# Six more weight slabs of a hybrid decoder block in the seven-product scheme, with its activation differences kept longer and one projection moved behind another

## The chip, the cores and the metric

The kernel runs on one core of a Trainium2 chip. The metric is the time of one execution on the device in microseconds (us). The kernel before took 943.69, 945.80 and 946.13 us in three runs, a median of 945.8. One further execution was profiled. Engines are called as in the profile: PE is TensorE, PEld its weight loads, DVE is VectorE, ACT is ScalarE, POOL is GpSimd, SP issues the transfers.

## What is computed

One layer on 512 tokens and 16 meta tokens (T = 528), model width 1024, all in float32. The input is normalised, multiplied by one wide matrix `w_in`, and cut into eight parts of 1024 columns. Four feed a retention branch, two a gated linear recurrence, two the gates by which the branches are mixed. A feed-forward network (FFN) follows.

```python
u = rmsnorm(h, mix_norm_w)
proj = u @ w_in
q, k, v, g_ret, lru_in, lru_gate, gate_a, gate_b = split(proj, split_at)
o = chunk_retention(rotary(q), rotary(k), v)            # normalised per head
y_ret = (silu(g_ret) * o) @ w_branch_ret
c = causal_depthwise_conv(lru_in, conv_w, conv_b)
r = rg_lru(c, lru_wa, lru_ba, lru_wx, lru_bx, lru_lambda)
y_lru = (gelu(lru_gate) * r) @ w_branch_lru
mixed = sigmoid(gate_a) * y_ret + sigmoid(gate_b) * y_lru
h = h + mixed @ w_out
u = rmsnorm(h, ffn_norm_w)
g, up = split(u @ w_ffn_in)
h = h + (silu(g) * up) @ w_ffn_out
```

In `rg_lru`, two small block-diagonal products of `c` give two sigmoid gates, from which the decay and the input of a recurrence over the tokens are made.

## The kernel before, in words

**Precision.** A float32 product is made of three: each operand is split into `hi` (rounded, by ACT, L290) and `lo` (the rest, by DVE, L294), and PE sums hi x hi, hi x lo and lo x hi into PSUM (`block`, L372 to L374, or `mm3`, L362 to L364).

**Weights.** A slab is 256 output columns of a weight matrix. It comes in four quarters of 128x512 elements: two halves of the depth, two halves of the columns. SP loads a quarter into one of eight `raw` buffers, ACT and DVE split it into one of nine pairs of `hi` and `lo`. `emit` does this for one piece; `weights` calls it up to eight pieces ahead of the one that PE uses next, in the order of the list `pieces`.

**Two ways to multiply a slab with the activations** (two halves of the depth by two halves of the tokens: `b11`, `b21`, `b12`, `b22`):

- Plain (`plain`, `plain512`): four pieces, eight blocks of 12 matmuls. A column half has one PSUM bank, which ACT reads at the end through the slab's function.
- Seven products (`fast`, `fast512`, and `fast528` where the meta tokens are wanted too), a Strassen scheme: POOL makes four sums of quarters, `s1` to `s4` (L260, `combine`), which with the quarters `a11`, `a12` and `a22` are seven pieces. PE multiplies them with four activation blocks or with the differences `t1` to `t4`, in seven blocks of 12 matmuls. After four blocks ACT copies two of the banks (L392, L394) and DVE adds one (`pz`, L393); only then may the last three blocks be summed into the same banks. At the end ACT copies one (L398), and DVE makes the result with two adds (L407, L408).

`t1` to `t4` are made once (`sums_of`), with hi and lo in eight of 32 slots of SBUF that all larger tiles share (`Slots`, `get`, `put`).

**Order of the work.** `PLAN` lists it. R0 to R3 are the retention's projections, A0 to A3 the gate `gate_a`, BR the product with `w_branch_ret`. I0 to I3 are the recurrence's input (`lru_in`), T0 to T3 its small gates and then its steps, L0 to L3 the gate `lru_gate`, B0 to B3 the gate `gate_b`, BL the product with `w_branch_lru`. In the trace these are the tiles `li`, `gt`, `lg` and `gate`, `w_br` and `w_bl`; a number behind li, lg or gate in the orders below counts the slabs of `w_in` (li16 is I0, lg20 is L0, gate28 is B0). The FFN's first product has `f` and `zwf`, `yxf`, its second `fo`.

Work of DVE, ACT and POOL that follows a projection is put off (`defer`) and mixed into PE's later work by `tick`: the convolution of an input slab (`conv`: per half of the slab one L978, three L980, one split at L422) and the recurrence (`recurrence`: POOL's L1019 and L1045, ACT's lookups, DVE's L1033 to L1047 and the product with the gate, L1052). Within an engine the build's scheduler then sets the order.

**Who is plain before.** K0 and G0, I2 and I3, L0 to L3, B0 to B3 (L217), and the first two FFN slabs. `t1` to `t4` are given back at BR.

Of the kernel before, what the change touches and what calls it, by code (L numbers as in the profile page):

```python
# [13 lines left out]
AF = mybir.ActivationFunctionType  # L14
# [6 lines left out]
SEQ = 512  # L21
# [41 lines left out]
FIRST_LOADS = "w0 x1 w1 m w2 w3 x2 x3"  # L63


PLAN = "R0 R1 R2 R3 A0 A1 A2 A3 I0 I1 BR T0 L0 I2 T1 L1 I3 L2 T2 B0 L3 T3 B1 B2 B3 BL"

PLAIN_R = "K0 G0".split()
NORM = 2.0
SUM = 2.0  # L70

# [39 lines left out]
class Slots:  # L111
# [12 lines left out]
    def get(self, n=SEQ, dt=F32):  # L124
        if n <= T and dt == F32:
            if self.halves:
                slot, i = self.halves.pop(0)
            else:
                slot, i = [*self.open(dt), 0], 0
                self.halves.append((slot, 1))  # L130
            slot[2] += 1
            t = slot[1][:, i * T:i * T + n]
            self.held[id(t)] = (t, slot, i)
        else:
            tag, mem = self.open(dt)
            t = mem[:, :n]
            self.held[id(t)] = (t, tag, None)
        return t

    def put(self, *tiles):  # L140
        for t in tiles:
            _, slot, i = self.held.pop(id(t))
            if i is None:
                self.free.append(slot)
                continue
            slot[2] -= 1
            self.halves.append((slot, i))
            if slot[2] == 0:
                self.halves = [h for h in self.halves if h[0] is not slot]
                self.free.append(slot[0])  # L150
# [3 lines left out]
def hybrid_block(ctx: ExitStack, tc: tile.TileContext, a: dict):  # L154
# [8 lines left out]
    get, put = slots.get, slots.put  # L163

    def bank(name):
        return ps.tile([P, 512], F32, tag="ps", name=name)
# [24 lines left out]
    Q, K, V, G, LI, LG, GA, GB = (4 * i for i in range(8))  # L191
# [4 lines left out]
    SLAB_OF = {"I": ("w_in", LI), "L": ("w_in", LG), "A": ("w_in", GA), "B": ("w_in", GB), "T": ("gates", 0)}  # L196
    for step in PLAN.split():
        if step in ("BR", "BL"):
            order += [(f"w_{step.lower()}", hf) for hf in range(2)]
        elif step[0] == "R":  # L200
            s = int(step[1])
# [12 lines left out]

    def plain_slab(key, i):
        if key == "w_in":
            return i in [{"Q": Q, "K": K, "G": G}[r[0]] + int(r[1]) for r in PLAIN_R] or LI + 2 <= i < GA or i >= GB  # L217
        return key == "w_fi" and i < FIRST

    pieces = []  # L220
# [18 lines left out]
    def behind(ins, other):  # L239

        if other is not None:
            tc.add_manual_dep(ins.ins, other.ins.name, mybir.DependencyInfo(
                mybir.DependencyClass.NoSync, mybir.DependencyReason.DATA), reason="issue order")
        return ins
# [74 lines left out]
    def lookup(*args, **kw):  # L319
        state["table"] = behind(nc.scalar.activation(*args, **kw), state.get("table"))  # L320
# [56 lines left out]
    def fast(key, s, X, n, banks, name):  # L377

        z, w_, y, x = banks
        own = n == TH
        ws = small.tile([P, TH], F32, tag="ws", name=f"ws{name}{s}")
        pz = small.tile([P, 2, TH], F32, tag="pz", name=f"pz{name}{s}")
        u2 = small.tile([P, TH], F32, tag="u2", name=f"u2{name}{s}")
        part = lambda name: weights((key, s, name))[0]
        block(z, part("s1"), X["t1"], n, True)
        block(w_, part("s3"), X["t3"], n, own)
        block(y, part("a12"), X["b21"], n, True)  # L390
        block(x, part("a11"), X["b11"], n, own)
        nc.scalar.copy(ws[:, :n], w_)  # L392
        nc.vector.tensor_tensor(pz[:, 1, :n], z, ws[:, :n], op=ALU.add)  # L393
        nc.scalar.copy(pz[:, 0, :n], x)  # L394
        block(z, part("s4"), X["b22"], n, False)
        block(w_, part("a22"), X["t4"], n, False)
        block(x, part("s2"), X["t2"], n, False)
        nc.scalar.copy(u2[:, :n], x)  # L398
        return pz, u2

    def fast512(key, s, X, out, name):

        zw, yx = bank(f"zw{name}{s}"), bank(f"yx{name}{s}")
        pz, u2 = fast(key, s, X, 256, (zw[:, :256], zw[:, 256:], yx[:, :256], yx[:, 256:]), name)
        out = out.rearrange("p (q n) -> p q n", n=256)
        halves = lambda t: t.rearrange("p (q n) -> p q n", n=256)
        nc.vector.tensor_tensor(out[:, 0::3], halves(yx), pz[:, :, :256], op=ALU.add)  # L407
        nc.vector.tensor_tensor(out[:, 1:3], halves(zw), u2[:, :256].unsqueeze(1).broadcast_to([P, 2, 256]), op=ALU.add)  # L408
# [25 lines left out]
    def plain(s, n, outs):  # L434


        shared = n == 256
        for j in range(2):
            for i, part in enumerate(PLAIN[2 * j:2 * j + 2]):
                w = weights(("w_in", s, part))[0]  # L440
                for h in range(2):
                    block(outs[j][h], w, UV[("b11", "b12", "b21", "b22")[2 * i + h]], n, i == 0 and (h == 0 or not shared))

    def plain512(s, name):

        pbs = [bank(f"{name}{s}_{j}") for j in range(2)]
        plain(s, 256, [(pb[:, :256], pb[:, 256:]) for pb in pbs])
        return pbs

    def branch(key, source, done):  # L450


        parts = {}
        for hf in range(2):
            acc = [bank(f"{key}{hf}_{c}") for c in range(4)]
            for k in range(KT):
                i = k // 2
                if i not in parts:
                    f = source(i)
                    parts[i] = get(D, F32R), get(D, F32R)  # L460
                    split(parts[i], f)
                    put(f)
                w = weights((key, i, k % 2 + 2 * (1 - hf)))[0]
                xh, xl = (p[:, k % 2 * SEQ:(k % 2 + 1) * SEQ] for p in parts[i])
                for c in range(4):
                    mm3(acc[c], *(p[:, c * P:(c + 1) * P] for p in w), xh, xl, k == 0, k == KT - 1)
                if hf == 1 and k % 2 == 1:
                    put(*parts.pop(i))
            for c in range(4):
                done(4 * hf + c, acc[c])  # L470
# [25 lines left out]
    def blocks_of(n):  # L496

        F = {b: get(4 * TH) for b in BLOCKS.values()}
        X = {b: (get(4 * TH, F32R), get(4 * TH, F32R)) for b in BLOCKS.values()}
        v4 = lambda t: t[:, :4 * n].rearrange("p (k t) -> p k t", k=4)  # L500
        return F, X, {b: v4(t) for b, t in F.items()}, {b: tuple(v4(t) for t in x) for b, x in X.items()}
# [40 lines left out]
    UF, U, UFV, UV = blocks_of(TH)  # L542
    for load in FIRST_LOADS.split():
        if load[0] == "w":
            key, i, c = pieces[int(load[1:])]
# [384 lines left out]
    def gated(T, base):  # L930


        def done(c, pb):
            s, j = c // 2, c % 2
            if j == 0:
                T[s] = get(D)
            sl = slice(j * SEQ, (j + 1) * SEQ)
            nc.vector.scalar_tensor_tensor(T[s][:, sl], sig[base, s][:, sl], 1.0, pb, ALU.add, ALU.mult)
            if j == 1:
                put(sig.pop((base, s)))  # L940
        return done

    def retained(i):
        for item in ret[i]:
            finish(item)
        return R[i]
# [108 lines left out]

    def lru_gate(s):
        x = get(D)
        for j, pb in enumerate(plain512(LG + s, "lg")):
            lookup(x[:, j * SEQ:(j + 1) * SEQ], pb, AF.Gelu_apprx_tanh)
        Z[s] = x  # L1060


# [20 lines left out]

    plan = PLAN.split()
    for step in plan:
        s = int(step[1]) if step[1:2].isdigit() else None
        if step[0] == "R":
            ret_project(s)
            if s == 0:
                softplus()  # L1090
            if s == 3:
                put(ropef)
        elif step == "BR":
            for i in range(4):
                retained(i)
            for b in ("t1", "t2", "t3", "t4"):
                put(*U.pop(b))
            branch("w_br", lambda i: R[i], gated(macc, GA))
        elif step == "BL":
            for b in ("b11", "b12", "b21", "b22"):  # L1100
                put(*U.pop(b))
            branch("w_bl", recurred, merged)
        elif step[0] == "A":
            gate(s, GA)
        elif step[0] == "B":
            gate(s, GB)
        else:
            {"I": lru_in, "T": lru_gates, "L": lru_gate}[step[0]](*(int(i) for i in step[1:]))
# [7 lines left out]
    def out_norm(t):  # L1116
# [3 lines left out]
        else:  # L1120
            diag, rows = None, get(D)
            held = rows
            nc.vector.tensor_scalar_mul(rows, h_sb[t], rms_factors(h_sb[t], f"h{t}", diagonal=False))
        yield NORM
        for c in range(2):
# [206 lines left out]
```

## Time and profile before

| what | value |
|---|---|
| three runs | 943.69, 945.80, 946.13 us |
| the profiled execution | 945.7 us, its span 943.9 us |
| granted PE clock, mean | 0.989 |
| busy in the span: PE, DVE, ACT, POOL | 918.9, 701.9, 468.7, 362.9 us |
| instructions | 16975 |
| moved by DMA | 91.5 MB, a mean of 97 GB/s |

A share of busy time is a mean over stages with different limits. The 40 slices of the page are 23.6 us each; a digit is the busy share in tenths. The recurrence's part, which the change edits, lies at about 304 to 536 us of the span.

### The profile page before, as it was taken

The page shows a single profiled execution, that of the slowest core. Times are in us where ns is not written, and L with a number is a line of the kernel's source. Part 1 is how long each engine was busy: PE and PEld are TensorE (multiplying, and loading weights), DVE is VectorE, ACT ScalarE, POOL GpSimd, SP SyncE. Part 2 cuts the span into 40 slices and gives each one's busy share as a digit, 9 for nine tenths or more (in the row PEclk, how much of TensorE's full clock was granted, in tenths as well). Part 3 has the DMA queues.
Part 4 walks back from the last instruction along what each step waited for, and adds up shares of the span by engine and source line. Part 5 has one row for each costly group of instructions (what it writes and reads, how often), then busy time and mean ns, then how long its engine had stood idle before and what let it go on. Part 6 is the DMA issues. An engine that isn't in the chain of part 4 may idle for free.

```text
span 943.9 us, 16975 instructions
## 1 busy us (share of the span) xinstructions
PE 918.9 (97%) x6562; PEld 862.7 (91%) x6562; DVE 701.9 (74%) x927; ACT 468.7 (50%) x823; POOL 362.9 (38%) x259
## 2 busy tenths in 40 slices
PE   8999899988999999999999999999999999999996
PEld 8999899988999889999998888999999999888885
DVE  5878996999788846887744527999999999832223
ACT  6654544545456327747933324554555556622213
POOL 6144654547351002112100214587887785000003
PEclk9999999999999999999999999999999999999999
DMA  7141122222123332232442222133333233432202
GB/s 276 57 141 62 57 85 85 74 84 68 56 80 124 122 102 79 84 108 91 147 132 90 93 87 78 56 111 104 102 98 124 92 99 124 135 102 91 88 1 90
DMA packets 48498, 91.50 MB, mean 97 GB/s; under 512 B 5520, under 2 KB 5648, under 8 KB 48416
## 3 DMA queue, kind: packets, MB, share of 16 engines
q1 hardware_dynamic: 46976, 86.70, 28.5%
q10 hardware_dynamic: 1440, 3.71, 1.2%
q8 instruction: 51, 0.84, 0.4%
q14 instruction: 31, 0.25, 0.1%
HBM read 88.29 MB, written 2.10 MB: 96 GB/s over the span
## 4 chain that ended last, share of the span: by engine, by line
PE 90%; DVE 6%; issue 2%; ACT 1%; DMA 0%; POOL 0%; POOLq 0%; DVEq 0%; ACTq 0%
PE fo L362 4%; PE fo L364 4%; PE fo L363 4%; PE zwf L372 4%; PE zwf L374 4%; PE zwf L373 4%; DVE lo L294 3%; PE yxf L372 3%; PE yxf L374 3%; PE yxf L373 3%; PE lg L374 2%; PE gate L374 2%; PE gate L372 2%; PE lg L372 2%; PE lg L373 2%; PE gate L373 2%
## 5 line engine op out<-in xcount | busy, mean ns | idle before, releaser
L294 DVE TENSOR_TENSOR lo<-raw_w_in,hi 128x512 fp32r<-128x512 f32 x96 | 82.6, 866 | 30.0 <-ACT hi L290 29.8
L372 PE MATMUL zwf<-b,hi 128*128 128x256 f32 x320 | 91.5, 287 | 2.2 <-DVE pzf L393 2.2
L373 PE MATMUL zwf<-b,hi 128*128 128x256 f32 x320 | 90.1, 282 | 0.0
L374 PE MATMUL zwf<-b,lo 128*128 128x256 f32 x320 | 90.0, 281 | 0.0
L294 DVE TENSOR_TENSOR lo<-s_w_fi,hi 128x512 fp32r<-128x512 f32 x80 | 83.8, 1084 | 1.3 <-ACT hi L290 0.8
L290 ACT CAST hi<-raw_w_in 128x512 fp32r<-128x512 f32 x96 | 58.9, 619 | 46.8 <-PE w_br L363 13.9
L294 DVE TENSOR_TENSOR lo<-raw_w_fo,hi 128x512 fp32r<-128x512 f32 x44 | 30.3, 692 | 64.4 <-ACT hi L290 64.4
L294 DVE TENSOR_TENSOR lo<-s_w_in,hi 128x512 fp32r<-128x512 f32 x64 | 64.3, 1014 | 11.8 <-ACT hi L290 9.5
L260 POOL TENSOR_TENSOR s_w_fi<-raw_w_fi,raw_w_fi 128x512 f32<-128x512 f32 x40 | 69.0, 1744 | 8.2 <-DVE lo L294 8.2
L362 PE MATMUL fo<-hi,b 128*128 128x512 f32 x176 | 69.4, 394 | 0.0
L363 PE MATMUL fo<-lo,b 128*128 128x512 f32 x176 | 68.8, 391 | 0.0
L364 PE MATMUL fo<-hi,b 128*128 128x512 f32 x176 | 68.2, 394 | 0.0
L294 DVE TENSOR_TENSOR lo<-raw_w_fi,hi 128x512 fp32r<-128x512 f32 x46 | 67.8, 1501 | 0.0
L372 PE MATMUL yxf<-b,hi 128*128 128x256 f32 x240 | 65.5, 281 | 2.2 <-ACT pzf L394 2.2
L373 PE MATMUL yxf<-b,hi 128*128 128x256 f32 x240 | 66.7, 280 | 0.0
L374 PE MATMUL yxf<-b,lo 128*128 128x256 f32 x240 | 66.6, 281 | 0.0
L372 PEld LDWEIGHTS zwf<-b,hi 128*128 128x128 f32 x320 | 60.7, 190 | 4.5 <-DVE pzf L393 3.2
L290 ACT CAST hi<-raw_w_fo 128x512 fp32r<-128x512 f32 x44 | 27.3, 621 | 73.7 <-PE fo L364 71.2
L290 ACT CAST hi<-s_w_in 128x512 fp32r<-128x512 f32 x64 | 39.6, 620 | 46.4 <-PE zwgate L373 8.0
L260 POOL TENSOR_TENSOR s_w_in<-raw_w_in,raw_w_in 128x512 f32<-128x512 f32 x32 | 46.2, 1452 | 42.1 <-DMA raw_w_in<-in_w_in 26.0
L374 PEld LDWEIGHTS zwf<-b,lo 128*128 128x128 f32 x320 | 61.0, 191 | 0.0
L373 PEld LDWEIGHTS zwf<-b,hi 128*128 128x128 f32 x320 | 60.9, 190 | 0.0
(412 smaller groups left out, 3312.0 us busy)
## 6 DMA issues: line engine op xcount, KB each, us to landing
raw_w_in<-in_w_in SPq DMA_DIRECT2D x112, 256.0 KB, 3.1
raw_w_fi<-in_w_fi SPq DMA_DIRECT2D x88, 256.0 KB, 3.3
raw_w_fo<-in_w_fo SPq DMA_DIRECT2D x44, 256.0 KB, 2.9
raw_w_v<-in_w_v SPq DMA_DIRECT2D x16, 256.0 KB, 4.6
raw_w_br<-in_w_br SPq DMA_DIRECT2D x16, 256.0 KB, 3.0
raw_w_bl<-in_w_bl SPq DMA_DIRECT2D x16, 256.0 KB, 3.0
raw_w_out<-in_w_out SPq DMA_DIRECT2D x16, 256.0 KB, 2.9
b<-in_x SPq DMA_DIRECT2D x4, 512.0 KB, 6.5
```

Of the source, the lines that this page charges most:

```text
L260: behind(nc.gpsimd.tensor_tensor(sums[key, i, name], x, y, op=op), state.get("diag"))
L290: nc.scalar.copy(hi, src)
L294: engine.tensor_tensor(lo, src, hi.bitcast(F32), op=ALU.subtract)
L362: nc.tensor.matmul(out, wh, xh, start=start, stop=False, skip_group_check=True)
L363: nc.tensor.matmul(out, wh, xl, start=False, stop=False, skip_group_check=True)
L364: nc.tensor.matmul(out, wl, xh, start=False, stop=stop, skip_group_check=True)
L372: nc.tensor.matmul(out, wh, xh, start=start and i == 0, stop=False, skip_group_check=True)
L373: nc.tensor.matmul(out, wh, xl, start=False, stop=False, skip_group_check=True)
L374: nc.tensor.matmul(out, wl, xh, start=False, stop=i == 3, skip_group_check=True)
```

## The change

Four places are edited.

- `PLAIN_L` names the plain slabs of the recurrence's part: I2, I3, L3 and B0 stay plain. L0, L1, L2, B1, B2 and B3 go over to seven products.
- `lru_gate` gets the branch for it: `fast512` into an SBUF tile, then one lookup of 1024 columns in place of two of 512. `gate`, for B, has this branch already.
- `t1` to `t4` are given back at BL, no longer at BR.
- I1 stands behind BR in the plan, no longer ahead of it.

```diff
-PLAN = "R0 R1 R2 R3 A0 A1 A2 A3 I0 I1 BR T0 L0 I2 T1 L1 I3 L2 T2 B0 L3 T3 B1 B2 B3 BL"
+PLAN = "R0 R1 R2 R3 A0 A1 A2 A3 I0 BR I1 T0 L0 I2 T1 L1 I3 L2 T2 B0 L3 T3 B1 B2 B3 BL"
 
 PLAIN_R = "K0 G0".split()
+
+PLAIN_L = "I2 I3 L3 B0".split()
...
     def plain_slab(key, i):
         if key == "w_in":
-            return i in [{"Q": Q, "K": K, "G": G}[r[0]] + int(r[1]) for r in PLAIN_R] or LI + 2 <= i < GA or i >= GB
+            return i in [{"Q": Q, "K": K, "G": G}[r[0]] + int(r[1]) for r in PLAIN_R] or i in [{"I": LI, "L": LG, "B": GB}[r[0]] + int(r[1]) for r in PLAIN_L]
...
     def lru_gate(s):
         x = get(D)
-        for j, pb in enumerate(plain512(LG + s, "lg")):
-            lookup(x[:, j * SEQ:(j + 1) * SEQ], pb, AF.Gelu_apprx_tanh)
+        if plain_slab("w_in", LG + s):
+            for j, pb in enumerate(plain512(LG + s, "lg")):
+                lookup(x[:, j * SEQ:(j + 1) * SEQ], pb, AF.Gelu_apprx_tanh)
+        else:
+            fast512("w_in", LG + s, UV, x, "lg")
+            lookup(x, x, AF.Gelu_apprx_tanh)
         Z[s] = x
...
         elif step == "BR":
             for i in range(4):
                 retained(i)
-            for b in ("t1", "t2", "t3", "t4"):
-                put(*U.pop(b))
             branch("w_br", lambda i: R[i], gated(macc, GA))
         elif step == "BL":
-            for b in ("b11", "b12", "b21", "b22"):
+            for b in list(U):
                 put(*U.pop(b))
             branch("w_bl", recurred, merged)
```

The orders of the two built programs differ on PE from the last blocks of I0 and the first of w_br to the first pass of w_bl; ahead of that and behind it they are the same. In sum the change has 72 matmuls of 128x256 fewer. DVE has 36 instructions more (18 lo, 6 pz, 12 adds), ACT 30 more (18 casts, 18 copies of 128x256, 6 lookups fewer), POOL 24 sums more. The transfers are as many as before.

In the orders shown below, source lines of the change are two higher than in the kernel before (L296 for L294, L395 for L393), `b` with a number is a tile in SBUF, and the number behind an underscore only counts tiles.

## Prediction

> **What bounds the kernel now.** I read the page first, for who is busy where.
>
> ```profile
> PE 918.9 (97%) x6562; PEld 862.7 (91%) x6562; DVE 701.9 (74%) x927; ACT 468.7 (50%) x823; POOL 362.9 (38%) x259
> PE   8999899988999999999999999999999999999996
> DVE  5878996999788846887744527999999999832223
> PE 90%; DVE 6%; issue 2%; ACT 1%; DMA 0%; POOL 0%; POOLq 0%; DVEq 0%; ACTq 0%
> ```
>
> TensorE (PE) holds 90% of the chain that ended last, so a matmul taken away is time taken away wherever PE never waits. VectorE (DVE) is the only other engine of weight. So I asked for the busy time by stage. The stages are the first w_br part (304:353), the recurrence's part that the change edits (353:491), w_bl behind it (491:536), and for comparison two parts that already run seven-product slabs: retention with its projections (100:250) and the FFN's first product (608:805). The columns are microseconds (us) of the window, then the busy time of PE, PEld, DVE, ACT and POOL, granted clock, DMA share and GB/s.
>
> ```profile
> 304.00:353.00 49.00, 49.00 (x232) 40.65 (x231) 34.14 (x58) 15.45 (x27) 0.00 (x0) 1.00 0.36 115
> 353.00:491.00 138.00, 138.00 (x1151) 138.00 (x1150) 98.17 (x133) 93.21 (x152) 24.00 (x12) 1.00 0.34 107
> 491.00:536.00 45.00, 45.00 (x197) 36.52 (x196) 18.58 (x24) 13.06 (x20) 5.33 (x4) 1.00 0.30 94
> 100.00:250.00 150.00, 140.78 (x1125) 137.05 (x1124) 132.76 (x187) 75.76 (x135) 79.77 (x51) 0.97 0.24 76
> 608.00:805.00 197.00, 194.47 (x1631) 191.99 (x1630) 194.24 (x193) 110.13 (x213) 152.32 (x94) 1.00 0.34 109
> 100.00:110.00 10.00, 7.63 (x52) 7.35 (x51) 10.00 (x13) 6.33 (x11) 4.70 (x3) 0.83 0.34 106
> ```
>
> In the edited part PE is busy for all 138.00 us at full clock: it waits for nothing there, and DVE has 39.8 us to spare. In the two comparison parts DVE is full (132.76 of 150, 194.24 of 197), and there PE does lose time: 9.2 us of 150 and 2.5 us of 197. What PE waited for there is in the waits of PE:
>
> ```profile
> PE zwq L372 <- DVE pzq L393: 4.0, 2, 3.7
> PE zk L372 <- DVE pzk L393: 2.4, 1, 2.4
> PE ktm L868 <- DVE km L817: 2.4, 1, 2.4
> PE zwf L372 <- DVE pzf L393: 2.2, 3, 1.0
> PE yxf L372 <- ACT pzf L394: 2.2, 2, 1.9
> ```
>
> It is hardly ever the weights' lo. It is pz, the hand-off in the middle of a seven-product slab: the second half accumulates into banks which DVE and ACT must read first, and that add stands in DVE's queue behind whatever was put there before. Plain slabs have no such hand-off.
>
> **What PE saves.** A plain slab is 8 blocks of 12 matmuls, a seven-product slab 7, so 72 matmuls of 128x256 go over six slabs. The tile view of the gate slabs B1 to B3 gives the pace:
>
> ```profile
> L372 PE MATMUL gate<-b,hi x96: 277/282/290, 456.8 to 490.7; 128*128 128x256 f32 x96
> L374 PE MATMUL gate<-b,lo x96: 280/282/285, 457.0 to 490.9; 128*128 128x256 f32 x96
> ```
>
> From the first start, 456.8, to the last, 490.9, lie 287 steps: 0.119 us each (the 0.28 us of one is overlap). So 72 x 0.119 = 8.6 us, all on the path. The profiled execution took 945.7 us (span 943.9 and 1.8 around it), 0.1 under the median of 945.8. With no new wait it would take 937.1.
>
> **What DVE, ACT and POOL get.** First the prices. Columns of the groups: count, busy us, mean ns of one, idle before and who ended it. From 353:491, DVE without much company, then one ACT row:
>
> ```profile
> L294 DVE TENSOR_TENSOR lo<-raw_w_in,hi 128x512 fp32r<-128x512 f32 x34 | 26.4, 780 | 13.4 <-ACT hi L290 13.4
> L1047 DVE TENSOR_TENSOR_SCAN b<-b,b 128x528 f32<-128x528 f32 x8 | 10.0, 1250 | 3.7 <-POOL b L1045 3.7
> L1033 DVE SCALAR_TENSOR_TENSOR b<-b,b 128x528 f32<-128x528 f32 x8 | 5.6, 706 | 8.2 <-ACT b L320 8.2
> L294 DVE TENSOR_TENSOR lo<-raw_w_bl,hi 128x512 fp32r<-128x512 f32 x8 | 5.4, 686 | 5.5 <-ACT hi L290 5.5
> L980 DVE SCALAR_TENSOR_TENSOR b<-b,vec,b 128x525 f32<-128x525 f32 x4 | 5.2, 1310 | 0.0
> ...
> L980 DVE SCALAR_TENSOR_TENSOR b<-b,vec,b 128x527 f32<-128x527 f32 x4 | 3.1, 770 | 0.1
> L980 DVE SCALAR_TENSOR_TENSOR b<-b,vec,b 128x526 f32<-128x526 f32 x4 | 3.1, 767 | 0.1
> L422 DVE TENSOR_TENSOR b<-b,b 128x528 fp32r<-128x528 f32 x4 | 2.8, 709 | 2.0 <-ACT b L421 1.9
> L978 DVE TENSOR_SCALAR b<-b,vec 128x528 f32<-128x528 f32 x4 | 2.2, 555 | 0.1
> L968 DVE COPY b<-li 128x8 f32<-128x8 f32 x8 | 1.3, 160 | 0.0
> ...
> L290 ACT CAST hi<-raw_w_in 128x512 fp32r<-128x512 f32 x34 | 20.7, 618 | 12.7 <-PE li L373 7.9 <-PE w_br L363 2.2 <-PE lg L373 1.8
> ```
>
> And from 180:283, where seven-product slabs run with POOL adding quarters beside DVE:
>
> ```profile
> L294 DVE TENSOR_TENSOR lo<-s_w_in,hi 128x512 fp32r<-128x512 f32 x30 | 32.4, 1094 | 4.7 <-ACT hi L290 4.2 <-PE zk L373 0.5
> L294 DVE TENSOR_TENSOR lo<-raw_w_in,hi 128x512 fp32r<-128x512 f32 x22 | 22.0, 1002 | 0.8 <-ACT hi L290 0.7
> L407 DVE TENSOR_TENSOR b<-yxgate,pzgate 128x512 f32<-128x512 f32 x3 | 2.0, 678 | 0.0
> L408 DVE TENSOR_TENSOR b<-zwgate,u2gate 128x512 f32<-128x512 f32 x2 | 1.4, 676 | 0.0
> L393 DVE TENSOR_TENSOR pzgate<-zwgate,wsgate 128x256 f32<-128x256 f32 x3 | 1.2, 415 | 0.0
> ...
> L260 POOL TENSOR_TENSOR s_w_in<-raw_w_in,raw_w_in 128x512 f32<-128x512 f32 x16 | 23.0, 1448 | 4.4 <-DVE lo L294 4.4
> ```
>
> A plain slab costs DVE 4 x 0.780 = 3.1 us. A seven-product one costs seven lo, pz and two adds: with POOL beside it 4 x 1.094 + 3 x 1.002 + 0.415 + 0.678 + 0.676 = 9.2, without contention 7 x 0.686 + 1.77 = 6.6. Six conversions so add 6 x 3.45 = 20.7 to 6 x 6.0 = 36.2 us.
>
> The move of I1 brings its DVE work into the part as well. The end of w_br on PE, before and then in the change (w_br1_3 is the last bank of w_br, gt0 the gates of T0, zli17 the input slab I1):
>
> ```order
> L363 MATMUL w_br1_3_4172<-b96_4124,hi157_4147 128x512
> L364 MATMUL w_br1_3_4172<-b95_4123,lo157_4148 128x512
> L362 MATMUL gt0_1_0_4331<-b84_3841,hi159_4193 128x264
> L363 MATMUL gt0_1_0_4331<-b85_3842,hi159_4193 128x264
> L364 MATMUL gt0_1_0_4331<-b84_3841,lo159_4194 128x264
> ```
>
> ```order
> L365 MATMUL w_br1_3_4009<-b92_3961,hi150_3984 128x512
> L366 MATMUL w_br1_3_4009<-b91_3960,lo150_3985 128x512
> L374 MATMUL zli17_4163<-b26_468,hi151_4026 128x264
> L375 MATMUL zli17_4163<-b27_469,hi151_4026 128x264
> L376 MATMUL zli17_4163<-b26_468,lo151_4027 128x264
> ```
>
> PE's 84 matmuls of I1 cost it the same on either side of w_br. On DVE I1 is seven lo, one pz and four adds with eight-column tails: 4.8 to 7.4, plus 0.415 + 4 x (0.415 + 0.160) = 2.7 (the 264-column adds priced by the 256-column row), together 7.5 to 10.1. Its convolution is half of L980, L978 and L422's 528-column rows: (5.2 + 3.1 + 3.1 + 2.8 + 2.2) / 2 = 8.2 us. Up to now it lay in w_br's 49 us, where DVE idles 14.9.
>
> So the part grows on PE by I1's 84 x 0.123 = 10.3 and shrinks by 8.6: 139.7 us. DVE's demand in it goes from 98.2 to between 98.2 + 20.7 + 7.5 + 8.2 = 134.6 (96%) and 98.2 + 36.2 + 10.1 + 8.2 = 152.7 (109%). The nine pieces made ahead of PE exist in both kernels and about cancel. DVE's 40 us of room, which hid all its work, is gone either way.
>
> POOL gets 24 + 4 sums at 1.448 = 40.5 on its 24.0: 64.5 of 139.7. ACT gets per slab three casts and three copies of half a bank (at most 0.618 each) and I1's ten: 93.2 + 22.2 + 6.2 = 121.6. Neither is full, but both are strictly in turn, and POOL's turn is new. Before, and then in the change (L1019 and L1045 are the recurrence's products, in the change two lines further down; s1 to s4 of slabs 21 and 22 are the sums of L1 and L2):
>
> ```order
> L1019 TENSOR_TENSOR b102_4330<-b102_4330,b83_3840 128x1056
> L1045 TENSOR_TENSOR b102_4330<-b102_4330,b101_4329 128x528 x2
> L1019 TENSOR_TENSOR b108_4690<-b108_4690,b88_4001 128x1056
> L1045 TENSOR_TENSOR b108_4690<-b108_4690,b107_4689 128x528 x2
> L1019 TENSOR_TENSOR b121_5205<-b121_5205,b109_4695 128x1056
> ```
>
> ```order
> L1047 TENSOR_TENSOR b99_4317<-b99_4317,b98_4316 128x528
> L262 TENSOR_TENSOR s1_w_in22_4871<-raw_w_in22_0_4867,raw_w_in22_1_4869 128x512
> L262 TENSOR_TENSOR s3_w_in22_4875<-raw_w_in22_2_4873,raw_w_in22_0_4867 128x512
> L262 TENSOR_TENSOR s2_w_in22_4877<-s1_w_in22_4871,raw_w_in22_2_4873 128x512
> L1047 TENSOR_TENSOR b99_4317<-b99_4317,b98_4316 128x528
> L262 TENSOR_TENSOR s4_w_in22_4881<-raw_w_in22_3_4879,s2_w_in22_4877 128x512
> ```
>
> The product waits for DVE's L1044, and now L2's weight sums are queued behind it; behind them stand ACT's cast, DVE's lo and PE. On DVE the hand-off of L2 (pzlg22) stands like this, behind the convolution of I3 (b117) and two pieces of B0 (w_in28):
>
> ```order
> L982 SCALAR_TENSOR_TENSOR b117_5107<-b115_4963,vec_70,b117_5107 128x527
> L296 TENSOR_TENSOR lo192_5101<-raw_gates2_1_5098,hi192_5100 128x512
> L970 COPY b115_4963<-li3_10_4967 128x8
> L982 SCALAR_TENSOR_TENSOR b117_5107<-b115_4963,vec_70,b117_5107 128x526
> L296 TENSOR_TENSOR lo193_5128<-raw_w_in28_2_5125,hi193_5127 128x512
> L980 TENSOR_SCALAR b117_5107<-b115_4963,vec_70 128x528
> L982 SCALAR_TENSOR_TENSOR b117_5107<-b115_4963,vec_70,b117_5107 128x525
> L296 TENSOR_TENSOR lo194_5150<-raw_w_in28_3_5147,hi194_5149 128x512
> L395 TENSOR_TENSOR pzlg22_5096<-zwlg22_5093,wslg22_5095 128x256
> ```
>
> There was no such row for L2 before. Seven such hand-offs (six slabs and I1) now stand in a full queue.
>
> What that costs PE no row of this part shows, so I take the two parts where DVE is as full: 2.5 of 197 us is 1.8 us over 139.7, and 9.2 of 150 is 8.6. A gain beyond the matmuls is excluded, since PE has no wait left to lose. The clock adds to the upper end: after a wait of 2.4 us its mean was 0.83 over 10 us, 1.7 us lost. I take **4.4 us**: below the middle, since the waits in retention come with rotations and copies (L817) which this part lacks, and above the FFN's, since the recurrence makes DVE wait for ACT and POOL (8.2 + 3.7 us of idle in the rows above). The eight slots which t1 to t4 keep leave fewer for the part; a writer may wait for an old reader, 0 to 3 us by L422's 1.9 us for ACT, and I count it within the 4.4. No DMA is added. So 945.7 - 8.6 + 4.4 = **941.5 us**.
>
> A rule bears on the price of lo. The Trainium skill, "SBUF — State Buffer", section "SBUF: two separate sides", says that a DVE instruction with two SBUF inputs and a GpSimd one exclude each other for the whole instruction. The FFN part tests it, its L294 alone (columns: DVE and POOL):
>
> ```profile
> 608.00:805.00 197.00, 141.41 (x118) 33.95 (x20) 1.00 0.34 109
> ```
>
> 118 lo at an undisturbed 0.686 are 81 us, and POOL was busy 152.3 us: 233 in 197 us. So lo is stretched (141.41 / 118 = 1.20 us), but the two did not take full turns.
>
> **The rivals.** *DVE keeps up* (chance 0.15): at 134.6 us it fits, and nine pieces ahead cover the waits. Then PE loses 0 to 1.8: about 938. For it: PE lost next to nothing in the FFN part with DVE 99% busy. Against it: that part has no recurrence.
>
> *The waits eat the saving* (0.20): at the retention part's rate 8.6 us come back: 945.7. For it: L2's hand-off, as shown, has the queue of that part.
>
> *DVE overflows, slower* (0.13): at 152.7 us plus its own idle for ACT and POOL, 11.9, it needs 164.6 of 139.7, 24.9 too many. Only what w_bl does not need at once can slide into it: all four results are due at three quarters of its first pass, 17 us, with 26.4 / 45 of that idle, 9.9 us. PE waits for 15.0: 952.1. It decides from 11.4 us of waits on. Against it: stretched lo are partly waiting, not work.
>
> *POOL and DVE in full turns* (0.02): 134.6 less 13.3 of PSUM readers, plus 64.5, is 185.8 of 139.7; after the same 9.9, 36 us fall on PE: 973. That is the Trainium skill's rule in full, against the FFN row.
>
> **How the numbers follow.** My forecast case (0.50) runs from 938.9 (1.8 us of waits) to 944. The 0.3% that a measurement of this kernel can tell from no change is 2.8 us: 942.9 to 948.6. Faster: 0.15 and 0.45 of the forecast, 0.60. Same: the other 0.05 and 0.19 of the eaten saving, 0.24. Slower: 0.13 + 0.02 and 0.01, 0.16. The range 937.5 to 948 leaves out the two slower cases and a little at the fast end.
>
> **What would show it.** Right: from w_br's end to w_bl's start about 144 us, PE busy some 140 of it, DVE over 95%, pzlg and pzgate (L395) at the top of PE's waits there, none over 3 us. Step by step: 6490 matmuls, their pace 0.119; lo from s_w_in near 1.0 us; everything before I0 and behind w_bl as it was. Wrong: PE waits over 9 us there, or weights' lo as what it waits for, or a lower clock in the part.

## The result, and the profile after

The changed kernel takes 957.21 us (median of four runs, 955.59 to 959.68), the kernel before, measured beside it, 945.0: a ratio of 1.0132, 95% interval 1.0114 to 1.0149. The forecast was 941.5, a faster kernel; the change made it slower, and the measured time lies above the range. The profiled execution is the fastest of the four: it took 955.59 us, its span is 953.8. All line numbers from here on are the change's, unless a kernel is said to differ.

The page of the change:

```profile
PE 913.2 (96%) x6490; PEld 854.5 (90%) x6490; DVE 739.1 (77%) x963; ACT 483.2 (51%) x853; POOL 400.5 (42%) x283
...
PE   8999999988999998798999999999999999999996
...
DVE  5878997999887659996796536999999999832223
```

The 72 matmuls are gone, 6562 less 6490. But in the slices 16, 17 and 19 of 23.8 us, PE has 8, 7 and 8 tenths where it had nines, and DVE falls to 6 and 7 in the 19th and 20th. Two windows follow. The first is w_br from the last block of I0 on (w_br itself begins at 293.0 us). The second goes from its end to the first matmuls of w_bl, which begin at 496.1:

```profile
299.00:342.00 43.00, 43.00 (x190) 35.01 (x189) 28.65 (x43) 11.54 (x20) 11.57 (x8) 1.00 0.28 90
```

```profile
342.00:497.40 155.40, 141.79 (x1133) 139.61 (x1131) 136.44 (x182) 108.05 (x185) 57.44 (x32) 0.98 0.25 81
```

PE works for 141.8 us there, about the 140 that were forecast, but it needs 155.4 us for it. (The 141.8 hold 3.4 us lost at half clock, see below, and lack three blocks of B3, some 4.3 us, which stand behind the first 25 matmuls of w_bl.) DVE is busy for 136.4 of the 155.4, 88%: it is not the full engine of the forecast. The waits of PE between 342 and 506 (total, times, longest):

```profile
PE zwlg L374 <- DVE pzlg L395: 6.8, 2, 3.7
PE gate L374 <- ACT b L322: 1.7, 1, 1.7
PE gt L364 <- DVE b L409: 1.6, 1, 1.6
PE li L376 <- DVE lo L296: 1.4, 1, 1.4
PE zwgate L376 <- DVE lo L296: 1.1, 1, 1.1
PE yxgate L374 <- ACT pzgate L396: 0.7, 1, 0.7
PE w_bl L365 <- DVE b L424: 0.2, 1, 0.2
```

Together 13.5 us; before there were none. Half of it is the hand-off pz of L0 and of L1. (The expectations below count a wait from the start of the last matmul to that of the next, some 0.3 us more each: 15.4 for the first seven waits.) Behind the two long ones PE runs slowly. Its timeline after L0's:

```profile
366.55 0.28 PE L374 MATMUL li<-b,hi 128*128 128x264 f32 x1
369.98 0.39 PE L374 MATMUL zwlg<-b,hi 128*128 128x256 f32 x1 [3.14 <-DVE pzlg L395]
...
371.15 0.41 PE L375 MATMUL zwlg<-b,hi 128*128 128x256 f32 x1
371.36 0.41 PE L376 MATMUL zwlg<-b,lo 128*128 128x256 f32 x1
...
373.92 0.34 PE L376 MATMUL zwlg<-b,lo 128*128 128x256 f32 x1
```

A step is 0.21 us in place of 0.12. The clock's record has half speed for 3.41 us here and for 3.41 us after L1's wait, 1.7 us lost each time. The window behind L1's wait, with a granted clock of 0.54:

```profile
404.50:408.00 3.50, 3.47 (x17) 3.48 (x18) 3.50 (x6) 3.47 (x7) 0.00 (x0) 0.54 0.23 74
```

The Trainium skill ("TensorE: Matmul & The Clock Gate", Part 1) puts the halving after at least one idle window of about 3.4 us. The traces do not agree: here it followed waits of 3.1 and 3.7 us, in no_sums (below) one of 2.8, in the FFN of the kernel before one of 1.9, and in five_pool (below) waits of 3.0 and 3.1 us were not followed by it.

The sum: 945.7 - 8.6 + 13.5 of waits + 3.4 of clock = 954.0, and 955.6 were measured. Most of the 1.6 us between them is what a wait costs beyond its idle time, since the next matmul no longer overlaps the last: with the 15.4 in place of the 13.5 the sum is 955.9.

### The profile page after: what moved, and what is told of

Same layout as the page of the kernel before. It is cut to its first block, busy times and chain, and to the rows that moved or that the text cites. A ratio compares the mean times of both kernels' runs of the same rounds, so it can differ in the third digit from the quotient of the medians.

```text
span 953.8 us, 16988 instructions
## 1 busy us (share of the span) xinstructions
PE 913.2 (96%) x6490; PEld 854.5 (90%) x6490; DVE 739.1 (77%) x963; ACT 483.2 (51%) x853; POOL 400.5 (42%) x283
## 4 chain that ended last, share of the span: by engine, by line
PE 49%; DVE 3%; ACT 1%; issue 1%; DMA 0%; POOLq 0%; POOL 0%; DVEq 0%; SPq 0%; ACTq 0%
PE fo L364 4%; PE fo L366 4%; PE fo L365 4%; PE zwf L374 4%; PE zwf L376 4%; PE zwf L375 4%; PE yxf L374 3%; PE yxf L375 3%; PE yxf L376 3%; DVE lo L296 2%; PE w_bl L365 2%; PE wo L364 2%; PE wo L365 2%; PE wo L366 2%; PE w_bl L366 2%; PE w_bl L364 1%
## 5 line engine op out<-in xcount | busy, mean ns | idle before, releaser
L262 POOL TENSOR_TENSOR s_w_in<-raw_w_in,raw_w_in 128x512 f32<-128x512 f32 x44 | 64.5, 1472 | 121.2 <-DMA raw_w_in<-in_w_in 70.2
L296 DVE TENSOR_TENSOR lo<-s_w_in,hi 128x512 fp32r<-128x512 f32 x88 | 83.8, 957 | 24.9 <-ACT hi L292 22.7
L296 DVE TENSOR_TENSOR lo<-raw_w_in,hi 128x512 fp32r<-128x512 f32 x90 | 81.8, 915 | 12.3 <-ACT hi L292 12.2
L296 DVE TENSOR_TENSOR lo<-s_w_fi,hi 128x512 fp32r<-128x512 f32 x80 | 84.9, 1097 | 1.3 <-ACT hi L292 0.8
L292 ACT CAST hi<-s_w_in 128x512 fp32r<-128x512 f32 x88 | 54.1, 619 | 60.7 <-PE w_br L365 6.5
L296 DVE TENSOR_TENSOR lo<-raw_w_fo,hi 128x512 fp32r<-128x512 f32 x44 | 30.3, 690 | 65.0 <-ACT hi L292 65.0
L292 ACT CAST hi<-raw_w_in 128x512 fp32r<-128x512 f32 x90 | 55.4, 619 | 37.0 <-PE w_br L365 5.7
L296 DVE TENSOR_TENSOR lo<-raw_w_fi,hi 128x512 fp32r<-128x512 f32 x46 | 67.7, 1500 | 0.0
```

The lines of the kernel that those rows point to most:

```text
L262: behind(nc.gpsimd.tensor_tensor(sums[key, i, name], x, y, op=op), state.get("diag"))
L292: nc.scalar.copy(hi, src)
L296: engine.tensor_tensor(lo, src, hi.bitcast(F32), op=ALU.subtract)
```

## The experiments

Two theories stood at the start: the hand-offs wait because DVE is over its capacity, or because something holds up single DVE instructions just ahead of them. The candidates for that were the move of I1 with its scarcer slots, ACT's queue, and POOL. Ratios are against the kernel before, measured beside each; each has its 95% interval. The medians of the kernel before were 944.8 to 946.0. "Waits" are PE's between 342 and 506, summed from the view.

### Which part of the change costs the time

**move_only** (nothing converted; I1 behind BR and t1 to t4 kept):

```diff
-PLAIN_L = "I2 I3 L3 B0".split()
+PLAIN_L = "I2 I3 L0 L1 L2 L3 B0 B1 B2 B3".split()
```

> The plan of the change (I1 behind w_br, t1 to t4 kept until w_bl) with none of the six slabs converted. Before is 945.0 us, the change 957.2. If the move and the scarcer slots are what makes the change slow, this takes 952 or more, with PE waits in the first 30 us behind w_br. If POOL's sums beside DVE's work are (my theory now), this is 944 to 947 and PE waits for nothing in the part. If only the number of DVE instructions counts, it is 945 to 948, since it adds I1's and one convolution's 14 to 18 us to 40 us of room.

946.13 us, ratio 1.0008 (0.9999 to 1.0018), no wait of PE. The move and the eight slots that stay taken cost nothing that can be measured as long as all six slabs are plain.

**three_b** (B1 to B3 alone converted) and **three_l** (L0 to L2 alone), both with the move:

```diff
-PLAIN_L = "I2 I3 L3 B0".split()
+PLAIN_L = "I2 I3 L0 L1 L2 L3 B0".split()       # three_b
+PLAIN_L = "I2 I3 L3 B0 B1 B2 B3".split()       # three_l
```

> Of the six slabs only B1, B2 and B3 are converted, L0 to L2 are plain; the plan is that of the change. PE saves 36 matmuls of 0.119 us, 4.3 us. By the theory of POOL's sums, the convolutions and POOL's long product L1019 are past by then but for the last recurrence, so little is lost: 940 to 944, at most 3 us of PE waits. By the move: 948 or more. By the number of DVE instructions alone: about 942, since DVE was 85% busy at B1 to B3.

> Only L0, L1 and L2 are converted; the plan is that of the change. PE saves 4.3 us. By the theory of POOL's sums (they fall together with convolutions, recurrences and L1019): PE waits of 10 us or more at the hand-offs of L0 and L1 with the clock halved twice, 950 to 954. If the losses of the change were spread evenly over six slabs: 951. By the move: 950 or more. If three slabs fit into DVE's room: 942.

three_b: 945.87, 1.0007 (0.9998 to 1.0017), waits 2.0. three_l: 957.73, 1.0139 (1.0122 to 1.0156), waits 9.3 and two half-clock stretches of 6.8 us each, twice as long as in the change. The loss against the kernel before is at L0 to L2. B1 to B3 only lose what they save: the forecast 4.3 us of matmuls do not appear in three_b's time. The windows 342 to 506, three_b's and then three_l's (DVE is the third number with a count):

```profile
342.00:506.00 164.00, 161.97 (x1272) 157.78 (x1271) 135.96 (x185) 111.14 (x186) 43.20 (x24) 1.00 0.34 112
```

```profile
342.00:506.00 164.00, 154.74 (x1220) 152.89 (x1219) 128.64 (x181) 109.53 (x182) 39.20 (x20) 0.96 0.32 101
```

DVE is busier in the kernel that waits less. How full DVE is does not decide.

### What holds up the hand-offs of L0 to L2

DVE, POOL and ACT in the change, ahead of L0's hand-off (L982 is the convolution's shifted tap, L1021 the recurrence's first product, L1035 another step of the recurrence):

```profile
357.61 7.17 DVE L982 SCALAR_TENSOR_TENSOR b<-b,vec,b 128x527 f32<-128x527 f32 x4
364.70 0.68 DVE L296 TENSOR_TENSOR lo<-raw_w_in,hi 128x512 fp32r<-128x512 f32 x1
365.30 2.46 DVE L982 SCALAR_TENSOR_TENSOR b<-b,vec,b 128x525 f32<-128x525 f32 x2
367.69 0.68 DVE L296 TENSOR_TENSOR lo<-raw_w_in,hi 128x512 fp32r<-128x512 f32 x1
368.29 0.70 DVE L1035 SCALAR_TENSOR_TENSOR b<-b,b 128x528 f32<-128x528 f32 x1
368.91 0.68 DVE L296 TENSOR_TENSOR lo<-raw_w_in,hi 128x512 fp32r<-128x512 f32 x1
369.51 0.41 DVE L395 TENSOR_TENSOR pzlg<-zwlg,wslg 128x256 f32<-128x256 f32 x1
...
357.10 2.94 POOL L1021 TENSOR_TENSOR b<-b,b 128x1056 f32<-128x1056 f32 x1
361.20 1.29 POOL L262 TENSOR_TENSOR s_w_in<-raw_w_in,raw_w_in 128x512 f32<-128x512 f32 x1 [1.17 <-DMA raw_w_in<-in_w_in]
362.45 1.76 POOL L262 TENSOR_TENSOR s_w_in<-s_w_in,raw_w_in 128x512 f32<-128x512 f32 x1
...
363.24 0.36 ACT L394 COPY wslg<-zwlg 128x256 f32<-128x256 f32 x1
```

ACT's copy is done at 363.60, but pz runs at 369.51: DVE works off its queue in order. In it four taps of I1's convolution take 7.17 us (one alone is 0.77), just where POOL runs the recurrence's product for T0 and two sums for L1. That is 4.1 us more than four taps alone, and PE waits for 3.1. It is the convolution that the move of I1 brought behind w_br: the move costs nothing alone, but its taps stand ahead of the first new hand-off.

**no_sums** (the 24 sums on POOL left out; the six slabs take raw quarters in their place, so their products are other ones):

```diff
+    SUMLESS = {"s1": 0, "s3": 2, "s4": 3, "s2": 1}
...
+    def bare(key, i):
+        return key == "w_in" and i in (LG, LG + 1, LG + 2, GB + 1, GB + 2, GB + 3)
...
-        elif c == "s1":
+        elif c == "s1" and not bare(key, i):
...
-        if c in ("s1", "s2", "s3", "s4"):
+        if c in SUMLESS and bare(key, i):
+            src = quarter(key, i, SUMLESS[c])
+        elif c in ("s1", "s2", "s3", "s4"):
```

> The change, but POOL makes none of the 24 sums for the six slabs: ACT and DVE split the raw quarters in their place, so those six slabs are computed from wrong weights. PE, ACT and DVE have the instructions of the change, only POOL and the sums' buffers are relieved. If POOL's sums (their lock on SBUF, and the queue behind L1045) cause the loss, most of it goes: 937 to 943 us, L980 (L982) back at 0.7 us. If the number of DVE instructions causes it, whatever POOL does, it stays at 953 or more with pzlg at the top of PE's waits.

947.21, 1.0018 (1.0004 to 1.0032), waits 5.2: the sums cost 10 us, though none of them runs on PE or DVE, and the seven lo per slab are still made. 947.2 is above the 937 to 943 expected, so the sums are not the whole loss. L0's hand-off does not wait any more; L1's still does, for 2.8 us. POOL and DVE there (seven lines further down: L989 is the tap, L1028 the product):

```profile
384.06 2.45 POOL L1028 TENSOR_TENSOR b<-b,b 128x1056 f32<-128x1056 f32 x1 [2.18 <-ACT b L329]
...
384.12 2.96 DVE L989 SCALAR_TENSOR_TENSOR b<-b,vec,b 128x526 f32<-128x526 f32 x1
...
388.20 0.75 DVE L989 SCALAR_TENSOR_TENSOR b<-b,vec,b 128x525 f32<-128x525 f32 x1
```

The clearest rows of the study: the tap was issued 0.06 us after POOL's product and ended 0.57 us after it, 2.96 us for what takes 0.75 alone. These rows fit a tap that was shut out for the whole length of POOL's instruction.

**conv_cast_dve** (DVE casts the convolution's hi, so that ACT's queue no longer waits for taps), **act_handoff** (for the six slabs ACT copies the second bank too, and DVE adds two copies behind PE's way) and **both** together:

```diff
-            split((ch3[:, j], cl3[:, j]), c3[:, j], engine=nc.gpsimd if j in C_POOL else nc.vector)
+            nc.vector.tensor_copy(ch3[:, j], c3[:, j])
+            nc.vector.tensor_tensor(cl3[:, j], c3[:, j], ch3[:, j].bitcast(F32), op=ALU.subtract)
```

```diff
-        nc.vector.tensor_tensor(pz[:, 1, :n], z, ws[:, :n], op=ALU.add)
+        if key == "w_in" and s in (LG, LG + 1, LG + 2, GB + 1, GB + 2, GB + 3):
+            zs = small.tile([P, TH], F32, tag="zs", name=f"zs{name}{s}")
+            nc.scalar.copy(zs[:, :n], z)
+            nc.vector.tensor_tensor(pz[:, 1, :n], zs[:, :n], ws[:, :n], op=ALU.add)
+        else:
+            nc.vector.tensor_tensor(pz[:, 1, :n], z, ws[:, :n], op=ALU.add)
```

> The change with the convolution's cast to hi made by DVE itself and no longer by ACT, so that ACT's queue never waits for DVE's taps; nothing else differs. The change is 957.2 us, before 944.8. If ACT's queue, held 5.8 to 6.8 us by that cast, is what makes the hand-off of L1 late, its PE wait of 3.9 us and the clock dip behind it (1.7 us) go: 950 to 953, although DVE has eight more instructions. If DVE alone is too full, it gets slower still: 958 or more.

> The change with one more ACT copy per converted slab: ACT copies both banks, and DVE adds the copies later, off PE's path. PE's second half then waits for ACT alone. If DVE's queue ahead of the add is the cause, the PE waits at pzlg (6.8 us) and the two clock dips (3.4 us) go: 947 to 950. If ACT's own queue is late as well (at L1 the first copy came 6 us after PE's first half), only L0's wait goes: 952 to 955. If the capacity of DVE is the cause, PE waits move on to lo: no change, 956 or more.

> The two edits together: the convolution's cast on DVE, and the hand-off by two ACT copies. If the two queues in turn are the whole loss, PE waits in the part fall under 5 us: 941 to 947. If DVE's capacity, stretched by POOL, is the floor, PE waits for lo instead: 950 or more.

959.63, 1.0149 (1.0132 to 1.0166); 957.46, 1.0119 (1.0104 to 1.0134); 958.94, 1.0135 (1.012 to 1.015). Waits 14.3, 11.6 and 12.5. With act_handoff PE no longer waits for DVE's pz but for ACT's copies, 3.7 and 2.6 us at L1 and L0. Neither DVE's add nor ACT's cast is the cause by itself, and taking both away does not help: ahead of L1's hand-off ACT itself waits for DVE, 7.3 us in act_handoff (for a tap, before the cast) and 4.8 in both (for L1060, the product with the gate).

**one_tap** (two of the three shifted taps left out, so the convolution is another one):

```diff
-            for i in range(1, 4):
+            for i in range(1, 2):
```

> The change with two of the convolution's three shifted taps left out (16 L980 of 0.68 us undisturbed, 11 us of DVE, up to 20 us as stretched in the change), so the convolution is computed wrongly. If DVE's time is what runs out, about all of the 12 us come back: 938 to 945. If it is POOL's sums whatever DVE does: 953 or more.

952.33, 1.0067 (1.0052 to 1.0082), waits 9.9. Twelve taps fewer in the part give 5 us back: DVE's queue ahead of the hand-offs counts, but is not all of it.

### Giving POOL's work to DVE

**products_dve** (the recurrence's two products on DVE), **sums_dve** (the 24 sums on DVE), **all_dve** (both):

```diff
-            nc.gpsimd.tensor_tensor(g, g, c, op=ALU.mult)
+            nc.vector.tensor_tensor(g, g, c, op=ALU.mult)
...
-                nc.gpsimd.tensor_tensor(g1, g1, t, op=ALU.mult)
+                nc.vector.tensor_tensor(g1, g1, t, op=ALU.mult)
```

```diff
-        behind(nc.gpsimd.tensor_tensor(sums[key, i, name], x, y, op=op), state.get("diag"))
+        engine = nc.vector if key == "w_in" and i in (LG, LG + 1, LG + 2, GB + 1, GB + 2, GB + 3) else nc.gpsimd
+        behind(engine.tensor_tensor(sums[key, i, name], x, y, op=op), state.get("diag"))
```

> The change with the recurrence's products (L1021, 1056 columns, four times; L1047, 528 columns, eight times) on DVE and no longer on POOL. DVE gets 4 x 1.2 + 8 x 0.6 = 9.6 us of work; POOL loses 4 x 2.6 + 8 x 1.65 = 23.6 us. If a POOL instruction shuts out DVE's instructions with two SBUF inputs for its whole length (one L982 beside L1021's 2.45 us took 2.96 us, undisturbed 0.68), DVE loses less than it gains: 950 to 955 against 957.2. If DVE's instruction count is what runs out: 962 to 967.

> The change with the 24 sums of the six slabs on DVE and no longer on POOL. DVE gets 24 x 0.6 = 14.4 us; POOL loses 24 x 1.29 = 31 us undisturbed. If POOL's instructions shut DVE out for their length: DVE's stretch of 29 us falls to about 12 us as without the sums, so DVE is about even or better off, and the queue behind POOL's product is gone: 949 to 957. If DVE's instruction count runs out: 965 to 972.

> Both moves: POOL has nothing left in the part but I1's four sums. DVE has 24 us more work than in the change, but no stretch. If the shutting out is the cause: DVE's clean work of 129 us becomes 153 in a part of 145 to 160, with no waits for POOL: 948 to 956. If the count: 975 or more.

951.77, 1.0074 (1.0059 to 1.0088); 952.66, 1.0081 (1.0066 to 1.0097); 953.81, 1.0095 (1.0079 to 1.011). Waits 10.2, 12.2 and 10.8. DVE gets 12, 24 or 36 instructions more, and the medians are 5.4, 4.6 and 3.4 us below the change's: that speaks against a bound by DVE's work alone, and is what an exclusion by POOL would give. But with no POOL at all in the part 8 us are still lost, so POOL is not the only cause. products_dve shows where else. PE's longest wait there, what ACT and DVE do ahead of it, and POOL:

```profile
PE gt L364 <- DVE b L409: 4.2, 1, 4.2
```

```profile
425.63 1.22 DVE L1054 TENSOR_TENSOR b<-b,b 128x1024 f32<-128x1024 f32 x1
426.76 0.76 DVE L982 SCALAR_TENSOR_TENSOR b<-b,vec,b 128x526 f32<-128x526 f32 x1
427.44 0.70 DVE L424 TENSOR_TENSOR b<-b,b 128x528 fp32r<-128x528 f32 x1
428.06 1.89 DVE L296 TENSOR_TENSOR lo<-raw_w_in,hi 128x512 fp32r<-128x512 f32 x3
429.86 0.68 DVE L409 TENSOR_TENSOR b<-yxlg,pzlg 128x512 f32<-128x512 f32 x1
...
426.56 0.36 ACT L400 COPY u2lg<-yxlg 128x256 f32<-128x256 f32 x1
...
427.19 3.88 POOL L262 TENSOR_TENSOR s_w_in<-raw_w_in,raw_w_in 128x512 f32<-128x512 f32 x1 [36.95 <-DMA raw_w_in<-in_w_in]
```

PE has finished L2 (ACT has read its last copy at 426.92), and the gates of T2 need the banks that L2's last two adds must empty first. Ahead of them in DVE's queue stand a product of 1024 columns, a tap and a split of I3's convolution and three pieces for the next slabs, each at its undisturbed length. Nobody holds DVE up; the order does. Here POOL is the one that is shut out: a sum of 1.27 us lasts 3.88.

**three_b_products** (three_b with products_dve's edit):

> B1 to B3 alone in seven products (945.9 us, the same as before), with the recurrence's products on DVE. PE saves 4.3 us against before; the 2.6 us of waits at the gates' slabs stood behind the last recurrence's products on POOL. If those go: 941 to 944, faster than before. If DVE's count runs out: 947 or more.

945.13, 1.0003 (0.9994 to 1.0012), waits 2.3: no difference from three_b, and not the 941 to 944 that were expected. Moving the products gains nothing at B1 to B3; that this is so because little POOL work stands beside their hand-offs is a reading, not a test.

### Count or place

The next four have the products on DVE and fewer slabs converted; P is "one place", S is "the number of DVE's instructions".

```diff
-PLAIN_L = "I2 I3 L3 B0".split()
+PLAIN_L = "I2 I3 L2 L3 B0".split()                # five_products: L2 plain
+PLAIN_L = "I2 I3 L0 L1 L3 B0 B1 B2 B3".split()    # l2_products: L2 alone
+PLAIN_L = "I2 I3 L1 L2 L3 B0 B3".split()          # l0_b12_products
+PLAIN_L = "I2 I3 L0 L1 L2 L3 B0 B3".split()       # b12_products
```

> The change with the recurrence's two products on DVE (products_dve) and L2 plain again, so five slabs converted. With six the PE waits were 11.5 us: 1.0 at L0, 2.9 at L1, 4.45 at the gates of T2 right behind L2, 3.0 to 3.9 at B1 to B3, and one dip of the clock. Theory P (the rest of the loss stands at one place, L2 and T2): with L2 plain that wait of 4.45 and the dip's 1.7 go; the saving is 5 x 1.43 = 7.1, about 6 of waits stay: near 944.5, same. Theory S (what is lost goes with DVE's count of instructions, wherever they stand): a sixth less of the waits, so 945.6 - 7.1 + 9.6 + 1.7: 949 to 950.

> Only L2 in seven products, the recurrence's products on DVE, the move of I1 kept. Theory P (the place): L2 by itself shows a wait of 3 to 4.5 us at the gates of T2, with or without a dip of the clock: 945.6 - 1.4 + 4 to 6, 948 to 950. Theory S (the count): DVE has some 25 us of room in the part, so next to no wait: 944 to 945.5.

> L0, B1 and B2 in seven products (L1, L2 and B3 plain), the recurrence's products on DVE. L0 costs 1.0 us of waits in products_dve, B1 and B2 1.5 together. Saving 3 x 1.43 = 4.3, waits 2 to 2.5: 943.4 to 944.2 if the slabs are independent of each other (P); 945 or more if each conversion loses what the six lost on average (S).

> Only B1 and B2 in seven products, the recurrence's products on DVE. With B1 to B3 and the products on DVE the waits were 1.5 and 1.5 us and the time that of the kernel before. If the waits stand at B3 and the first of w_bl (P), B1 and B2 keep 2.9 less at most 1.5: 943 to 944.3. If they spread over the slabs (S): within 0.5 us of the kernel before.

| kernel | us | ratio (95%) | waits |
|---|---|---|---|
| five_products | 943.68 | 0.9977 (0.9968 to 0.9987) | 3.0 |
| l2_products | 948.68 | 1.0041 (1.0027 to 1.0054) | 3.2 |
| l0_b12_products | 942.08 | 0.9970 (0.9960 to 0.9980) | 0 |
| b12_products | 943.17 | 0.9983 (0.9974 to 0.9992) | 0 |

It is the place, from both sides: L2 alone makes the kernel slower, and the other five make it faster. What L2 does there is less clear. The waits of l2_products are:

```profile
PE gate L374 <- ACT b L322: 1.3, 1, 1.3
PE zwlg L374 <- DVE pzlg L395: 1.0, 1, 1.0
PE gt L364 <- DVE b L970: 0.9, 1, 0.9
```

The wait for L2's last two adds (L409), which was 4.2 us in products_dve and was expected here, is not among them. So that wait is not a matter of L2 alone; what else it needs was not separated. Windows 342 to 506 of five_products, and then of l2_products:

```profile
342.00:506.00 164.00, 160.87 (x1257) 156.50 (x1256) 146.42 (x210) 116.50 (x197) 27.25 (x16) 1.00 0.34 112
```

```profile
342.00:506.00 164.00, 160.84 (x1281) 157.79 (x1280) 123.10 (x184) 106.14 (x175) 9.36 (x4) 1.00 0.34 110
```

PE loses the same 3.1 us, once with DVE busy for 146 us, once for 123.

**five_pool** and **l0_b12_pool** (PLAIN_L as in five_products and l0_b12_products, the products left on POOL as in the change):

> The change with L2 plain again and nothing else, so the recurrence's products stay on POOL. Saving 5 x 1.43 = 7.1 us. If L2 alone is the cause (its sums, its pieces and the gates of T2 behind it), the hand-offs of L0 and L1 wait no longer than with the products on DVE: 943 to 945. If POOL's products shut DVE out by themselves, the waits of 3.4 us at L0 and of up to 3.9 at L1 stay, each with a dip of the clock of 1.7: 945.5 - 7.1 + 7 to 10: 946 to 949.

> The change with L1, L2 and B3 plain again, the recurrence's products on POOL: beside l0_b12_products (942.1, no PE wait in the part) it shows whether products on DVE are needed there. L0 is followed by a plain L1, so no sums fall beside its hand-off. If the waits need sums and products together: 941.5 to 942.5. If the products alone do it, 2 to 3.4 us of wait and a dip at L0: 944 to 947.

949.81, 1.0048 (1.0033 to 1.0064), and 942.69, 0.9972 (0.9960 to 0.9984). five_pool's longest waits:

```profile
PE zwlg L374 <- DVE pzlg L395: 6.2, 2, 3.1
```

All its waits are 8.2 us, and its clock is not halved in the part. The hand-offs of L0 and L1 wait beside POOL's products also when L2 is plain. So there are two causes, and in the times they add up:

| | products on POOL | products on DVE |
|---|---|---|
| L2 in seven products | 957.2 (the change) | 951.8 |
| L2 plain | 949.8 | 943.7 |

The columns differ by 5.4 and 6.1 us, the rows by 7.4 and 8.1. The profiles account for the 7.4 of the first column: 13.5 - 8.2 = 5.3 us more waits and 3.4 of clock, less the 1.4 that L2 saves, are 7.3. Of the 5.3, 3.3 are the two waits right behind L2 (the gates of T2, then B0). The 3.4 of clock follow L0's and L1's waits, which are nearly as long in five_pool, so it is not shown that L2 causes them. l0_b12_pool has no wait at all: L0 is followed by a plain L1 there, and one product of POOL without the sums of a next slab is absorbed. The best kernel measured is l0_b12_products, 3.4 us faster than the kernel before (interval 1.9 to 3.8 us by its ratio); l0_b12_pool is as good within the measurement.

## Why the prediction was wrong, point by point

- *What PE saves*: right. 6490 matmuls, PE busy for 141.8 us from w_br to w_bl, and l0_b12_products, which has no wait, ran 3.4 us faster for three slabs at a forecast 1.43 each, and b12_products, also without a wait, 2.3 for two. Both are a little less than forecast.
- *The move of I1 and the slots*: right to count them at little by themselves; move_only shows 0.08%, and its interval includes no change. But I1's convolution, which the move put into the part, is what stands in DVE's queue ahead of L0's hand-off.
- *Where PE would wait*: right in part. pzlg is at the top, but at L0 and L1 and with 3.1 and 3.7 us, where none was to be over 3; DVE's pz of the gate slabs is not among the waits. The queue that the text showed, L2's with the convolution of I3 and pieces of the next slab, ran at its undisturbed lengths and did not delay L2's pz (at 426.2 us; PE needed it at 427.9), but the last two adds behind it (a wait of 1.6 us here, 4.2 in products_dve). The text had the rows of that queue in hand and did not price them. Its own signs of being wrong, waits over 9 us and a lower clock in the part, both came.
- *DVE's demand*, 134.6 to 152.7: inside the range, 136.4 busy up to 497 us and 145.0 up to 506, but 88% of the time in both and not over 95%. Lo took 0.854 and 0.900 us against the 1.002 and 1.094 taken from retention:

```profile
L296 DVE TENSOR_TENSOR lo<-raw_w_in,hi 128x512 fp32r<-128x512 f32 x34 | 28.9, 854 | 4.0 <-ACT hi L292 4.0
L296 DVE TENSOR_TENSOR lo<-s_w_in,hi 128x512 fp32r<-128x512 f32 x24 | 21.5, 900 | 6.4 <-ACT hi L292 6.3
```

- *The step that failed*: "What that costs PE no row of this part shows, so I take the two parts where DVE is as full". It gave 4.4 us; 13.5 of waits and 3.4 of clock were measured. In all the change lies 18.5 us above the 937.1 that it would take with no new wait. Its premise is that waits go with how full DVE is. three_b against three_l, and five_products against l2_products, show that they do not: they go with what stands ahead of a hand-off in DVE's queue, and with how long POOL stretches it. The FFN part has no convolution and no recurrence in that queue.
- *The rivals*: "DVE overflows" had the sign, with 15.0 us of waits, but its mechanism is not what happened: DVE was idle for 12% of the part, and its 136.4 us lie far below the 152.7 of that rival. That the number of its waits is near is chance.
- *The rule that was rejected*: the Trainium skill, "SBUF — State Buffer", section "SBUF: two separate sides", was right as to the exclusion: the tap of 2.96 us beside the product of 2.45 agrees with it. The test on the FFN part was faulty. It added POOL's busy 152.3 us to DVE's undisturbed 81; but POOL's busy time holds POOL's own waiting for DVE. FFN's sums in the change, from the page, and then one sum for `w_in` from the change's timeline, beside a DVE add that reads PSUM:

```profile
L262 POOL TENSOR_TENSOR s_w_fi<-raw_w_fi,raw_w_fi 128x512 f32<-128x512 f32 x40 | 69.1, 1746 | 8.2 <-DVE lo L296 8.2
```

```profile
434.77 1.27 POOL L262 TENSOR_TENSOR s_w_in<-raw_w_in,raw_w_in 128x512 f32<-128x512 f32 x1 [0.46 <-DMA raw_w_in<-in_w_in]
```

  At 1.27 each POOL's 94 instructions would be 119 us (an estimate that takes the 20 lo made on POOL as long as a sum), with 81 just 200 of 197: the row does not speak against full turns. What was off in that rival is its price, 973. Some waiting was counted twice in it, since its 1.448 us for a sum and the tap of 1.310 us in its rows were stretched already; how much each term was too large is not shown.
- *The size of the clock's share*: one stretch of 1.7 us was reckoned in the upper end; there were two.

Left open: whether L0 would wait without the move of I1, since the change was not run without it; why some waits near 3 us are followed by half clock and others are not; how much of products_dve's gain is the exclusion and how much that the product itself is shorter on DVE and the recurrence so earlier; and whether L2 could be converted if its two last adds stood earlier in DVE's queue, which was not tried.

## What to carry to other kernels

Do not price a new hand-off by how full the engine is in another part. Read the queue row by row ahead of that one instruction, add up the undisturbed durations and the stretches by POOL, and compare that with the time that PE has until it needs the bank. And convert slab by slab: here three of the six places (L2 and the gates behind it, L0 and L1 beside POOL's products and sums) lost more than all six saved. Reading the queue like this was not tried here as a forecast.

## What the runs showed of the hardware that was not expected

- A DVE instruction with two inputs in SBUF and a POOL instruction shut each other out, in both directions: a tap of 0.75 us took 2.96 beside a product of 2.45, a sum of 1.27 us took 3.88 beside DVE's lo. So an engine's busy time in a trace can be waiting, and giving the recurrence's products from POOL to the busier DVE made the kernel 5.4 us faster than the change.
- Waits of PE of 3.1 and 3.7 us were each followed by 3.41 us at half clock, 1.7 us lost. It is not a fixed price: after waits of 3.0 and 3.7 us in three_l the clock was halved for 6.8 us each, and after two of 3.0 and 3.1 in five_pool not at all.
